# A channel-attention kernel whose two small warm-up tiles move from the front of the on-chip memory to its end

## The chip, the core and the metric

The kernel runs on one core of a Trainium2 chip. The core has a matrix engine (PE, with its weight loads listed apart as PEld), a vector engine (DVE), a scalar engine (ACT), a general engine (POOL) and a sync engine (SP) that here only issues transfers. All of them work on SBUF, an on-chip memory of 128 partitions; every buffer has one byte address that holds in all partitions. Sixteen DMA engines move data between HBM and SBUF. The metric is the device time of one execution in microseconds (us).

## The reference

Q, K and V have 8 batches, 12 heads, 512 rows and 64 columns in float32. For each of the 96 heads, Q and K are normalised along the rows, a 64 x 64 matrix of their products goes through a softmax, and V is multiplied by it:

```python
Q_norm = Q / (np.linalg.norm(Q, axis=-2, keepdims=True) + 1e-10)
K_norm = K / (np.linalg.norm(K, axis=-2, keepdims=True) + 1e-10)
attn = np.einsum('bhnd,bhne->bhde', Q_norm, K_norm)
attn = np.exp(attn - np.max(attn, axis=-1, keepdims=True))
attn = attn / (np.sum(attn, axis=-1, keepdims=True) + 1e-10)
return np.einsum('bhnd,bhde->bhne', V, attn).astype(np.float32)
```

Q, K and V are 12.6 MB each, and so is the result; all of it crosses the DMA engines once.

## The kernel before

**Work and staging.** Four heads make a unit (24 units), two units a step `s` (12 steps), and two steps a group `w` (6 groups). Q and K of a step land side by side in a float32 tile `qk32` (three buffers of 16 KB in each partition); V lands in `v32` (three of 8 KB). DVE casts Q and K to bfloat16 (`cast_qk`, L204); PE makes the products of a unit (`grams`, L224); DVE, ACT and POOL take the norms out of them, scale, and form the softmax (`squares` to `normalise`, L231 to L282); PE transposes V (`vtrans`, L293) and multiplies it by the weights (`outs`, L310); and ACT or DVE copies the result into a float32 tile `so` (`ocopy`, thirteen buffers of 4 KB), from which it is stored.

**Transfers.** All large transfers are issued by SP: `load_qk` (L180, L182, L184), `load_v` (L191, L193) and `store` (L198). A DMA packet carries one run of bytes that is contiguous in a partition and in HBM. From the shapes in those lines:

- Loads of V carry 8 KB in a packet, the last two 4 KB.
- Loads of Q and K carry 4 KB in a packet, those of the last unit 2 KB.
- Stores carry 2 KB in a packet (eight rows of 64 floats), the last two 1 KB.

**Order.** A small planner (`Order.run`) runs while the program is built. It holds a cost for each piece of work and writes out one order for each engine's queue. SP's queue is in order too; at most eight transfers are under way at a time, and the ninth waits for the first.

**The small reads.** Before everything else, ACT issues two transfers of 128 pieces of 64 bytes, one from Q and one from K, into two tiles `first0` and `first1`. No later instruction reads them.

**Addresses.** Buffers are given addresses in the order in which pools are opened and tiles are made in them. The first pool is `const`, and the tiles made first in it are `first0` and `first1`: they stand at bytes 16512 and 16576 and together take 128 bytes. Behind them come `ident`, `identb`, `eye2`, the four `ab` tiles, and then the other pools in the order of `NB`. A list of some of them:

| buffer | bytes in a partition | address before | remainder by 256 |
|---|---|---|---|
| first0, first1 | 64 each | 16512, 16576 | 128, 192 |
| ident | 512 | 16640 | 0 |
| ab (four) | 1024 each | 17664 and on | 0 |
| qk32 (three) | 16384 each | 21760, 38144, 54528 | 0 |
| v32 (three) | 8192 each | 70912, 79104, 87296 | 0 |
| vb, qkb, vt | 8192, 4096, 8192 | 95488, 111872, 120064 and on | 0 |
| so (thirteen) | 4096 each | 136448 and on | 0 |
| scr, kq (two each) | 2048 each | 189696 and on | 0 |
| kqs (two) | 2048 each | 198080, 200128 | 192 |
| ex (two) | 1024 each | 202240, 203264 | 0 |

Within a `qk32`, `v32` or `so` buffer the runs of all packets begin at multiples of 1 KB, so the address of the buffer sets where each packet begins within a block of 256 bytes.

Of the kernel before, what the change touches and what calls it, by code (L numbers as in the profile page):

```python
# [8 lines left out]
F32 = mybir.dt.float32  # L9
# [4 lines left out]
D = 64  # L14
# [88 lines left out]
def kernel(  # L103
# [36 lines left out]
    const = ctx.enter_context(tc.tile_pool(name="const", bufs=1))  # L140
# [4 lines left out]
    vtp = ctx.enter_context(tc.tile_pool(name="vtp", bufs=NB["vt"]))  # L145
    sop = ctx.enter_context(tc.tile_pool(name="sop", bufs=NB["so"]))
    small = ctx.enter_context(tc.tile_pool(name="small", bufs=NB["sm"]))
    ps_v = ctx.enter_context(tc.tile_pool(name="ps_v", bufs=1, space=bass.MemoryType.PSUM))
    ps_l = ctx.enter_context(tc.tile_pool(name="ps_l", bufs=1, space=bass.MemoryType.PSUM))
    ps_o = ctx.enter_context(tc.tile_pool(name="ps_o", bufs=2, space=bass.MemoryType.PSUM))  # L150
# [167 lines left out]


    for i in range(2):  # L320
        first = const.tile([128, D // 4], F32, name=f"first{i}")
        nc.scalar.dma_start(out=first, in_=(Q, K)[i][0, 0, :128, :D // 4])

    nc.scalar.add_instruction(mybir.InstLoadActFuncSet(
        name=nc.get_next_instruction_name(), engine=mybir.EngineType.Activation, ins=[], outs=[], act_func_set_id=LN_EXP))
# [102 lines left out]
    for s in range(S):  # L428
        for x in range(4):
            i, k = divmod(x, 2)  # L430
# [57 lines left out]
```

## Time and profile before

| what | value |
|---|---|
| median of 13 runs | 128.86 us (128.64 to 129.61) |
| the profiled execution's own time | 128.74 us |
| its span, first to last instruction | 127.0 us |
| DVE busy | 94.2 us (74% of the span) |
| PE busy, ACT busy, POOL busy | 72.9, 72.5, 38.6 us |
| DMA packets, bytes | 15893, 50.66 MB |
| mean DMA rate | 399 GB/s |
| share of 16 DMA engines' span taken by the large transfers' packets | 98.6% |

The span leaves out 1.74 us of the execution (128.74 less 127.0), which lies before its first and after its last instruction. In the slices of the page each digit stands for a fortieth of the span, 3.2 us; the rows named DMA and GB/s tell how busy the DMA engines were in it and how much they moved. In the list of DMA queues, q1 is SP's queue with the large transfers, q10 is ACT's with the two small reads, and q8 and q14 are fetches of the program itself.

### The profile page before, as it was taken

How to read it: one execution, taken by the hardware profiler on the slowest of the kernel's cores; microseconds unless marked ns; L12 is line 12 of the kernel's file. 1: busy time of each engine (PE TensorE's matmuls, PEld its weight loads, DVE VectorE, ACT ScalarE, POOL GpSimd, SP SyncE). 2: the span in 40 equal slices, each digit the busy share in tenths (PEclk: the TensorE clock that was granted, in tenths of full speed). 3: DMA queues.
4: the chain of work that ended last, by engine and by line, in shares of the span. 5: the costliest groups of instructions: out<-in, count | busy, mean ns of one | idle time of the engine just before them, and what ended most of it. 6: DMA issues, size and time to landing. Idle time of an engine off the chain costs nothing.

```text
span 127.0 us, 4885 instructions
## 1 busy us (share of the span) xinstructions
PE 72.9 (57%) x2128; PEld 59.1 (47%) x2128; DVE 94.2 (74%) x141; ACT 72.5 (57%) x220; POOL 38.6 (30%) x39
## 2 busy tenths in 40 slices
PE   0074087396583386855972689582977786853000
PEld 0063075285462275744852468371856574742000
DVE  3445756939999989997899999998999887960000
ACT  4000303557969209967386589877668997896000
POOL 4006307040833830432074301413473370300000
PEclk9999999999999558997799999999589997698555
DMA  4999999999999999999999999999999999999993
GB/s 136 378 431 418 421 416 418 416 428 413 422 427 413 413 414 426 403 421 421 428 412 416 410 425 418 416 431 414 408 407 417 397 407 399 404 403 407 407 373 127
DMA packets 15893, 50.66 MB, mean 399 GB/s; under 512 B 1408, under 2 KB 1920, under 8 KB 14464
## 3 DMA queue, kind: packets, MB, share of 16 engines
q1 hardware_dynamic: 15584, 50.34, 98.6%
q8 instruction: 16, 0.26, 0.7%
q10 hardware_dynamic: 288, 0.02, 0.2%
q14 instruction: 5, 0.04, 0.1%
HBM read 37.77 MB, written 12.58 MB: 397 GB/s over the span
## 4 chain that ended last, share of the span: by engine, by line
DVE 34%; PE 24%; issue 12%; DMA 11%; ACT 9%; POOL 1%; DVEq 0%; ACTq 0%; POOLq 0%
DVE qkb L204 16%; PE gram L224 12%; DMA qk<-in_K_dram 8%; DVE scr L231 6%; PE vps L293 5%; PE po L310 5%; DVE ab L282 5%; DVE vt L167 3%; DMA first<-in_Q_dram 3%; ACT so L165 3%; ACT vt L165 2%; PE lg L267 2%; ACT ex L273 2%; DVE n L243 2%; ACT kq L165 1%
## 5 line engine op out<-in xcount | busy, mean ns | idle before, releaser
L224 PE MATMUL gram<-qkb 32*128 32x128 bf16 (+1 forms) x1504 | 32.6, 242 | 28.1 <-DVE qkb L204 16.1
L204 DVE CAST qkb<-qk 128x1024 bf16<-128x1024 f32 x48 | 41.8, 897 | 5.6 <-DMA qk<-in_Q_dram 3.1
L224 PEld LDWEIGHTS <-qkb 32*128 32x128 bf16 (+1 forms) x1504 | 27.3, 107 | 32.3 <-DVE qkb L204 17.3
L169 POOL TENSOR_SCALAR vb<-v 128x1024 bf16<-128x1024 f32 x19 | 23.4, 1248 | 30.3 <-DMA v<-in_V_dram 29.4
L165 ACT COPY so<-po 128x512 f32<-128x512 f32 x45 | 24.9, 593 | 7.3 <-PE po L310 6.8
L254 POOL TENSOR_TENSOR kqs<-kq,r 64x512 f32<-64x512 f32 x12 | 13.9, 1158 | 40.4 <-issue 19.3
L165 ACT COPY vt<-vps 128x1024 bf16<-128x1024 bf16 (+1 forms) x18 | 17.8, 987 | 13.0 <-PE vps L293 12.8
L310 PE MATMUL po<-ab,vt 128*64 128x128 bf16 x384 | 19.4, 237 | 5.7 <-issue 1.8
L293 PE MATMUL vps<-identb,vb 128*128 128x128 bf16 x192 | 18.2, 248 | 7.1 <-DVE vt L167 2.5
L231 DVE SCALAR_TENSOR_TENSOR scr<-gram,eye 64x512 f32<-64x512 f32 x24 | 16.5, 688 | 5.8 <-PE gram L224 5.5
L293 PEld LDWEIGHTS <-vb 128*128 128x128 bf16 x192 | 13.9, 111 | 10.3 <-issue 6.2
L310 PEld LDWEIGHTS <-vt 128*64 128x64 bf16 x384 | 13.5, 118 | 10.2 <-issue 5.1
L273 ACT ACTIVATE ex<-lg,rq 128x64 f32<-128x64 f32 x48 | 14.5, 323 | 4.0 <-PE lg L267 4.0
L165 ACT COPY kq<-gram 64x512 f32<-64x512 f32 x12 | 7.0, 581 | 14.0 <-DVE scr L231 13.8
L282 DVE TENSOR_TENSOR ab<-ex,rinv 64x256 bf16<-64x256 f32 x24 | 12.3, 512 | 0.6
L273 ACT ACTIVATION_READ_ACCUMULATOR ex<-lg,rq 128x1 f32 x48 | 10.3, 214 | 0.0
L167 DVE COPY vt<-vps 128x1024 bf16<-128x1024 bf16 (+1 forms) x8 | 8.0, 1023 | 2.0 <-PE vps L293 1.9
L243 DVE TENSOR_REDUCE n<-scr 128x8 f32<-128x512 f32 x12 | 8.2, 680 | 0.1
L267 PE MATMUL lg<-eye,kqs 64*128 64x64 f32 x48 | 6.4, 258 | 1.9 <-POOL kqs L254 1.0
L267 PEld LDWEIGHTS lg<-eye,kqs 64*128 64x128 f32 x48 | 4.5, 156 | 3.6 <-issue 1.4
L167 DVE CAST vb<-v 128x1024 bf16<-128x1024 f32 x5 | 5.0, 1002 | 0.1
L279 DVE RECIPROCAL rinv<-esum 128x4 f32<-128x4 f32 x12 | 2.0, 170 | 3.9 <-ACT ex L273 3.9
(16 smaller groups left out, 15.8 us busy)
## 6 DMA issues: line engine op xcount, KB each, us to landing
out_dram<-so SPq DMA_DIRECT2D x23, 512.0 KB, 10.2
v<-in_V_dram SPq DMA_DIRECT2D x11, 1024.0 KB, 17.3
qk<-in_Q_dram SPq DMA_DIRECT2D x8, 1024.0 KB, 15.1
qk<-in_K_dram SPq DMA_DIRECT2D x8, 1024.0 KB, 16.9
qk<-in_Q_dram SPq DMA_DIRECT2D x8, 512.0 KB, 11.6
qk<-in_K_dram SPq DMA_DIRECT2D x8, 512.0 KB, 11.5
v<-in_V_dram SPq DMA_DIRECT2D x2, 512.0 KB, 10.7
out_dram<-so SPq DMA_DIRECT2D x2, 256.0 KB, 9.3
```

Of the source, the lines that this page charges most:

```text
L165: nc.scalar.copy(o, i)
L167: nc.vector.tensor_copy(o, i)
L169: nc.gpsimd.tensor_scalar(out=o, in0=i, scalar1=1.0, scalar2=0.0, op0=ALU.mult, op1=ALU.add)
L204: nc.vector.tensor_copy(qkb[u][:, :, x * D:(x + 1) * D], qk32[s][:, x, r])
L224: nc.tensor.matmul(gram[s][:, h, r, 0], x, x, start=(t == 0), stop=(t == (T if u < WIDE else J) - 1))
L231: nc.vector.scalar_tensor_tensor(out=scr[s][half], in0=gram[s][half, :, :, 0, half].rearrange("p h r d -> p (h r) d"), scalar=1e-20, in1=e ...
L254: (nc.vector if eng == "DVE" else nc.gpsimd).tensor_tensor(out=kqs[s][HI], in0=kq[s][HI], in1=r8[s][HI, :, None].to_broadcast([D, 2 * HU, ...
L267: nc.tensor.transpose(l[:, h, :], kqs[s][HI, 2 * h:2 * h + 2].rearrange("p r d -> p (r d)"), eye2[HI])
L273: nc.scalar.activation(e[:, h, :], lg[s][:, h, :], AF.Exp, scale=rq[s][:, h:h + 1], accum_out=z[:, h:h + 1])
L282: nc.vector.tensor_tensor(out=a[half, :, half], in0=e[half], in1=ri[half, :, None].to_broadcast([D, HU, D]), op=ALU.mult,)
L293: nc.tensor.transpose(ps[:, c, n, :], vb[w][:, J * c + j].rearrange("p r d -> p (r d)"), identb)
L310: nc.tensor.matmul(po[s, x][e * D:(e + 1) * D, j].rearrange("p r d -> p (r d)"), v, ab[s][:, h, :])
```

## The change

A new pool `endp` is opened behind `small`, the last pool of SBUF, and `first0` and `first1` are made in it and no longer in `const`:

```diff
     sop = ctx.enter_context(tc.tile_pool(name="sop", bufs=NB["so"]))
     small = ctx.enter_context(tc.tile_pool(name="small", bufs=NB["sm"]))
+    endp = ctx.enter_context(tc.tile_pool(name="endp", bufs=1))
     ps_v = ctx.enter_context(tc.tile_pool(name="ps_v", bufs=1, space=bass.MemoryType.PSUM))
...
     for i in range(2):
-        first = const.tile([128, D // 4], F32, name=f"first{i}")
+        first = endp.tile([128, D // 4], F32, name=f"first{i}")
         nc.scalar.dma_start(out=first, in_=(Q, K)[i][0, 0, :128, :D // 4])
```

All other buffers move down by 128 bytes: `ident` now stands at 16512, `qk32` at 21632, `v32` at 70784, `so` at 136320 and on. The remainders by 256 that were 0 are now 128; that of `kqs` goes from 192 to 64. The two small tiles stand at 204288 and 204352, with remainders 0 and 64. No engine's list of instructions changes, neither the order nor a shape nor what any instruction waits for.

## The prediction

> **What bounds the kernel now.** I read the slices first, then the DMA queues, then the chain of waits, and last the stretch in which nothing but stores is left. The slices of the page:
>
> ```profile
> DVE  3445756939999989997899999998999887960000
> DMA  4999999999999999999999999999999999999993
> GB/s 136 378 431 418 421 416 418 416 428 413 422 427 413 413 414 426 403 421 421 428 412 416 410 425 418 416 431 414 408 407 417 397 407 399 404 403 407 407 373 127
> ```
>
> DVE is busiest of the computing engines, but it has gaps and it is done four slices before the end. The DMA engines are at 9 in every slice but the first and the last. The queues say the same in one number:
>
> ```profile
> DMA packets 15893, 50.66 MB, mean 399 GB/s; under 512 B 1408, under 2 KB 1920, under 8 KB 14464
> q1 hardware_dynamic: 15584, 50.34, 98.6%
> q8 instruction: 16, 0.26, 0.7%
> q10 hardware_dynamic: 288, 0.02, 0.2%
> ```
>
> The packets of SP's transfers took 98.6% of what sixteen engines have in the span. The counts "under" are cumulative. Minus the 1408 tiny ones (the small reads and the completion marks), 512 packets are of 1 KB; 14464 less 1920 are of 2 or 4 KB; the rest, but for 21 fetches of the program, are the 1408 of 8 KB. With the shapes of the lines that is 6400 of 2 KB (5888 in stores, 512 in the last loads), 6144 of 4 KB, 1408 of 8 KB: in all 14464 packets that carry data, 904 for each engine. 6400 of them (5888 and 512) leave an `so` buffer, 8064 enter `qk32` or `v32`.
>
> The chain of waits tells another story at first sight:
>
> ```profile
> DVE 34%; PE 24%; issue 12%; DMA 11%; ACT 9%; POOL 1%; DVEq 0%; ACTq 0%; POOLq 0%
> ```
>
> It follows engine instructions through their semaphores, and a store that sits in a full queue has no place in it. What is decisive is the end. The stretches of 12 us (columns: time, length, busy time of PE, PEld, DVE, ACT, POOL, clock, DMA share, GB/s), and then a shorter one in the drain:
>
> ```profile
> 16.00:28.00 12.00, 8.77 (x232) 7.28 (x236) 7.72 (x13) 4.02 (x15) 3.69 (x3) 1.00 1.03 421
> ...
> 100.00:112.00 12.00, 9.16 (x200) 7.41 (x194) 9.59 (x17) 10.64 (x40) 4.55 (x4) 0.86 1.05 403
> ```
>
> ```profile
> 118.00:122.00 4.00, 0.00 (x0) 0.00 (x0) 0.00 (x0) 0.00 (x0) 0.00 (x0) 0.50 1.05 406
> ```
>
> In the last stretch no engine computes and only 2 KB (and the last 1 KB) stores run: the transfers that were queued drain, at the DMA engines' own pace. The last store is issued at 117.1 us and lands 9 us later. So the end is set by the sum of packet times on the DMA engines, from some 3 us on to 126, with hardly a hole. A packet that takes 1 ns longer moves the end by 904 ns if all are hit; a computing engine that gets faster or slower by little moves nothing.
>
> **What a packet costs.** The trace's packet records have nearly one time for each size: 11 ns for 64 bytes, 46 for 1 KB, 84 for 2 KB, 159 for 4 KB, 309 for 8 KB (medians). (309 - 159) ns for 4096 bytes are 1.172 ns for 32 bytes; I call that a beat. 9 ns and a beat for every 32 bytes fits all five. Neighbouring packets overlap by a few ns, which is why the DMA share above is over 1: at 406 GB/s an engine passes 25.4 bytes in a ns, so a 2 KB packet holds it for 80.7 ns. The completion marks take 16 x 9 ns for 256 packets of a store, 0.6 each; that leaves 80.1, of which 64 beats are 75.0 and 5.1 are the packet's own.
>
> **The change part by part.**
>
> Order, waits, issues: nothing. SP issues the same 70 transfers, ACT the same two small reads, ahead of the table load at L324 as before; nothing is added or moved on any queue. The pool at the end adds no wait, since nothing reads its tiles.
>
> The small reads' new places (0 and 64 in a block of 256 bytes, before 128 and 192): 256 packets of 11 ns on 16 engines are 0.18 us in total, while the first large loads are only starting. Were each 4 beats shorter or longer, it would be 16 x 4.7 = 75 ns. I take 0.
>
> The computing engines: every operand's address falls by 128 bytes, and the distances between buffers stay. The trace has no pair of one operation at both remainders. I bound it by the busiest row, DVE's 48 casts of 897 ns in the mean, 41.8 us: 1% either way is 0.4 us, hidden behind a DMA queue that had no hole even in 64 to 76 us, where DVE is busy for 11.8 of 12 us. To lose that cover the casts would have to slow so much that a load is issued late by more than the queue holds (a load of Q and K takes 11 to 17 us from issue to landing). I take 0.
>
> The packets' SBUF ends: this is where the change acts. All 14464 packets now begin 128 bytes into a block of 256 in SBUF; their ends in HBM stay. [...] I weigh it for the two directions.
>
> - *Stores* read SBUF. [...] 400 x 4.7 = 1.88 us. The trace holds no store from such an address; from below the price is 0 (the beats are hidden in the packet's own 5.1 ns), and a gain is bounded in the rivals.
> - *Loads* write SBUF; what they read in HBM is aligned as before. The nearest row is that of the small reads, q10 above: they do write at 128 and 192 bytes into a block, and take 11 ns, where the line through the other sizes gives 9 + 2 x 1.172 = 11.3. Had a write to pay for the bytes ahead of it, it would be 4.7 to 7 ns more, 16 to 18. So I take 0 for 8064 packets, against 504 x 4.7 = 2.36 us if loads paid like stores. The row doesn't settle it wholly: a 64-byte packet crosses no block, and a 4 KB one now touches 17 in place of 16. A beat for each additional block would be 504 x 1.172 = 0.59 us.
>
> The sum against the profiled execution's 128.74 us (span 127.0 and 1.74 around it): +1.88, so 130.6. The median of the runs shown is 0.12 above that execution; so 130.7. A second number follows for the drain: 80.7 + 4.7 = 85.4 ns for a packet, so some 384 GB/s where 406 stood.
>
> **The rivals.**
>
> *Loads pay too.* [...] Against it: the 11 ns of the small reads. 14464 packets, 904 on an engine, x 4.7 = 4.24 us: 133.1.
>
> *Only the additional block costs*, a beat or so on every packet: 904 x 1.172 = 1.06 us, 129.9. [...] Against it: nothing in the trace shows a beat for a block.
>
> *Nothing is seen*: the beats hide, and the kernel is not slower. [...] A 2 KB packet holds the engine for 80.1 / 1.172 = 68.3 beats, of which 64 move data[...]. The 4 additional beats fit into exactly that; it decides as soon as the surplus is 4.3 beats or less. [...] It gives 128.9[...].
>
> *Faster.* The packets' own 5.1 ns could become less at the new addresses. If one beat of it went on all packets, -1.06 us: 127.8. For it: I know of no row that says the old remainder is the best. Against it: five sizes lie on one line, and the 64-byte packets at other remainders lie on it too, so an effect of the old remainder on the fixed part isn't visible.
>
> *Far slower*: if each half-filled block broke the stream on both ends, 10 beats or more a packet, 904 x 11.7 = 10.6 us and more, over 139. Only possible, no row points to it.
>
> **How the numbers follow.** Stores pay 4 beats: 0.36. Loads too: 0.17. A beat for a block: 0.10. Far slower: 0.04. Nothing seen: 0.21. Faster: 0.12. The runs before can tell about 0.3% (0.4 us) from no change. Slower by more is 0.36 + 0.17 + 0.10 + 0.04 = 0.67, within it 0.21, faster 0.12. The likeliest is 130.7; its own range is 130.0 to 131.2 (room for one to two of the beats, or half a beat for the loads' blocks). The range of 8 in 10 has to reach down to no change and up to the case where loads pay as well: 128.5 to 133.3, which leaves out faster and far slower, 0.16.
>
> **What would show it.** Right: packets of 2 KB in the drain at about 384 GB/s, while the stretch from 16 to 28 us keeps its 421; a 2 KB packet of a store takes some 88 to 89 ns, and 4 and 8 KB ones stay at 159 and 309; the mean durations of casts, copies and matmuls stay. Wrong: 421 falls to some 410 early on (loads pay); 406 stays (nothing seen); a DMA row with holes while an engine's means have moved (then it's the computing engines, which I priced at nothing).

## The result, and the profile after

The changed kernel takes 130.35 us in the median (11 runs, 129.96 to 131.19); the kernel before, now over 48 runs, 129.06 us (128.62 to 130.05). The ratio is 1.011, with a 95% interval of 1.0086 to 1.0135: slower by 1.3 us. The profiled execution has 130.15 us and a span of 128.4, where the one before had 128.74 and 127.0.

The number is close to the forecast of 130.7, but the profile says that it came from elsewhere. The same rows as before, of the changed kernel; first the slices and the queues:

```profile
DVE  3443849919999989999977779999999789850000
DMA  4999999999999999999999999999999999999993
GB/s 128 392 435 408 421 407 406 408 420 405 411 425 407 403 407 411 404 415 424 414 412 407 415 417 421 405 429 405 405 408 403 398 402 403 401 406 408 407 363 116
DMA packets 15893, 50.66 MB, mean 395 GB/s; under 512 B 1408, under 2 KB 1920, under 8 KB 14464
q1 hardware_dynamic: 15584, 50.34, 98.4%
q8 instruction: 16, 0.26, 0.8%
q10 hardware_dynamic: 288, 0.02, 0.2%
```

Bytes and packets are the same, the DMA row is as full, and the mean rate has gone from 399 to 395 GB/s. So the same packets took longer. Which ones, the stretches tell (columns as before; the last number is GB/s):

```profile
16.00:28.00 12.00, 8.39 (x248) 7.16 (x244) 7.75 (x12) 4.70 (x15) 4.07 (x4) 0.77 1.03 411
...
118.00:122.00 4.00, 0.00 (x0) 0.00 (x0) 0.00 (x0) 0.00 (x0) 0.00 (x0) 0.50 1.05 408
```

In the drain, where only stores run, 408 GB/s stand where 406 stood: nothing is slower. Early on, where only loads run, 421 fell to 411. The forecast had these two the other way round. A longer stretch, almost wholly of loads, serves as the yardstick from here on; the kernel before, then the changed one:

```profile
28.00:52.00 24.00, 14.73 (x492) 12.04 (x480) 22.24 (x31) 16.07 (x51) 8.79 (x7) 0.86 1.02 418
```

```profile
28.00:52.00 24.00, 16.61 (x454) 13.62 (x443) 22.55 (x32) 15.76 (x51) 9.12 (x8) 0.71 1.02 411
```

The packet records put it in figures. "Late" is the share of packets over the common 84, 159 or 309 ns; "sum" is what all packets of that size took, divided by 16 engines.

| packets on SP's queue | before: mean, late, sum | after: mean, late, sum |
|---|---|---|
| 2 KB (stores, last loads) | 84.4 ns, 2%, 33.78 us | 84.7 ns, 6%, 33.87 us |
| 4 KB (loads) | 161.4 ns, 2%, 61.97 us | 163.2 ns, 38%, 62.65 us |
| 8 KB (loads) | 310.2 ns, 1%, 27.29 us | 314.6 ns, 59%, 27.68 us |

The differences of the sums are 0.09, 0.68 and 0.39, together 1.16 us for an engine, of the 1.4 by which the span grew. The loads bear 1.07 of it, and not as one surcharge on each packet: 62% of the 4 KB packets still take exactly 159 ns, nearly all others 160 to 172.

One execution of each kernel would not settle this by itself, for executions of one kernel spread by as much (128.62 to 130.05 us for the kernel before). The change shows in the medians, and in a stretch towards the end of the drain; the kernel before, then the changed one:

```profile
122.00:124.00 2.00, 0.00 (x0) 0.00 (x0) 0.00 (x0) 0.00 (x0) 0.00 (x0) 0.50 0.90 340
```

```profile
122.00:124.00 2.00, 0.00 (x0) 0.00 (x0) 0.00 (x0) 0.00 (x0) 0.00 (x0) 0.50 1.06 402
```

In the kernel before, some of the DMA engines are already done there (DMA share 0.90, where the drain had 1.05); in the changed one all are still at work (1.06). Of the other full kernels, shown below, the four whose load buffers start at multiples of 256 move 314 to 340 GB/s in these two microseconds, the two whose load buffers do not 391 and 404.

The chain of waits names the transfers now, because it happens to follow the stores at the end:

```profile
DMA 27%; PE 25%; DVE 25%; issue 8%; ACT 5%; SPq 1%; ACTq 0%; DVEq 0%
```

The row of the casts guards against a wrong reading of the computing engines; the kernel before, then the changed one:

```profile
L204 DVE CAST qkb<-qk 128x1024 bf16<-128x1024 f32 x48 | 41.8, 897 | 5.6 <-DMA qk<-in_Q_dram 3.1
```

```profile
L205 DVE CAST qkb<-qk 128x1024 bf16<-128x1024 f32 x48 | 37.9, 813 | 7.0 <-DMA qk<-in_Q_dram 4.7
```

The mean of the casts is 813 ns where it was 897; it is no mark of the addresses, since it goes from 759 to 905 ns in the kernels below, and 905 belongs to a kernel in which the casts' results have the changed remainder and their inputs the old one. PE's busy time rose from 72.9 to 78.8 us at a lower mean clock (0.800 for 0.892). Neither casts nor PE set the end: the DMA engines were full in both executions (98.6 and 98.4% of their time in the span went to packets of SP's queue).

### The profile page after: what moved, and what is told of

Read it like the earlier page. It is cut to its first block, busy times and chain, and to the rows that moved or that the text cites. A ratio compares the mean times of both kernels' runs of the same rounds, so it can differ in the third digit from the quotient of the medians.

```text
span 128.4 us, 4885 instructions
## 1 busy us (share of the span) xinstructions
PE 78.8 (61%) x2128; PEld 64.3 (50%) x2128; DVE 93.6 (73%) x141; ACT 72.5 (56%) x220; POOL 36.6 (29%) x39
## 3 DMA queue, kind: packets, MB, share of 16 engines
q1 hardware_dynamic: 15584, 50.34, 98.4%
## 4 chain that ended last, share of the span: by engine, by line
DMA 27%; PE 25%; DVE 25%; issue 8%; ACT 5%; SPq 1%; ACTq 0%; DVEq 0%
DMA out_dram<-so 21%; PE gram L225 14%; DVE qkb L205 10%; DVE scr L232 5%; DMA qk<-in_K_dram 5%; PE vps L294 5%; PE po L311 5%; DVE ab L283 4%; ACT so L166 3%; DVE n L244 2%; DVE vt L168 2%; PE lg L268 1%; ACT ex L274 1%; DVE so L168 1%; SPq L185 1%
## 5 line engine op out<-in xcount | busy, mean ns | idle before, releaser
L225 PE MATMUL gram<-qkb 32*128 32x128 bf16 (+1 forms) x1504 | 37.4, 264 | 24.5 <-DVE qkb L205 10.4
L225 PEld LDWEIGHTS <-qkb 32*128 32x128 bf16 (+1 forms) x1504 | 31.8, 119 | 29.0 <-DVE qkb L205 12.8
L205 DVE CAST qkb<-qk 128x1024 bf16<-128x1024 f32 x48 | 37.9, 813 | 7.0 <-DMA qk<-in_Q_dram 4.7
L170 POOL TENSOR_SCALAR vb<-v 128x1024 bf16<-128x1024 f32 x19 | 21.7, 1153 | 39.5 <-DMA v<-in_V_dram 35.3
L166 ACT COPY vt<-vps 128x1024 bf16<-128x1024 bf16 (+1 forms) x18 | 17.7, 986 | 16.9 <-PE vps L294 16.7
L311 PE MATMUL po<-ab,vt 128*64 128x128 bf16 x384 | 20.6, 248 | 5.3 <-issue 2.9
L311 PEld LDWEIGHTS <-vt 128*64 128x64 bf16 x384 | 14.5, 124 | 10.0 <-issue 6.3
L283 DVE TENSOR_TENSOR ab<-ex,rinv 64x256 bf16<-64x256 f32 x24 | 15.1, 631 | 0.6
L168 DVE CAST vb<-v 128x1024 bf16<-128x1024 f32 x5 | 5.5, 1096 | 0.1
```

The costliest lines, as they stand in the source:

```text
L166: nc.scalar.copy(o, i)
L168: nc.vector.tensor_copy(o, i)
L170: nc.gpsimd.tensor_scalar(out=o, in0=i, scalar1=1.0, scalar2=0.0, op0=ALU.mult, op1=ALU.add)
L205: nc.vector.tensor_copy(qkb[u][:, :, x * D:(x + 1) * D], qk32[s][:, x, r])
L225: nc.tensor.matmul(gram[s][:, h, r, 0], x, x, start=(t == 0), stop=(t == (T if u < WIDE else J) - 1))
L283: nc.vector.tensor_tensor(out=a[half, :, half], in0=e[half], in1=ri[half, :, None].to_broadcast([D, HU, D]), op=ALU.mult,)
```

## The experiments

All addresses below were moved by empty tiles placed ahead of a pool (and a second one behind it, to bring what follows back to its old remainder). "Off the block" means that a buffer starts some bytes behind a multiple of 256. Ratios are to the kernel before, run on the same chip in the same session (129.09, 129.57 and 129.28 us in the three sessions). The kernels without computing are compared with one another by their times. The last four of them ran in a later session and on another chip than the first two; the very last, whose packets were all on time, gives a base there (127.01 us beside 127.05).

**Which buffers? Four kernels.** The small reads alone behind everything, with a gap of 128 bytes in their old place:

```diff
     const = ctx.enter_context(tc.tile_pool(name="const", bufs=1))
+    const.tile([128, 32], F32, name="gap")
...
-        first = const.tile([128, D // 4], F32, name=f"first{i}")
+        first = endp.tile([128, D // 4], F32, name=f"first{i}")
```

> The small reads stand behind all other buffers, and a gap of 128 bytes takes their old place, so that every other buffer keeps its old address. Theory that a packet which loads into SBUF from 128 bytes into a block is at times delayed: ratio 1.000 (within 0.002), 8 KB packets at a mean of 310 ns as before. Rival that the place of the small reads matters: 1.010.

Measured: 129.1 us against 129.09, ratio 0.9999 (0.9979 to 1.002); 8 KB packets at a mean of 310.5 ns. Its profiled execution is one of the longer ones (130.03 us), and yet its loads run as before:

```profile
28.00:52.00 24.00, 18.39 (x488) 15.55 (x490) 18.02 (x30) 16.22 (x50) 8.89 (x8) 0.71 1.02 418
```

Where the small reads stand is of no account; the move matters through the addresses of the others alone. It also shows the cure: the order of the buffers costs nothing here once a gap restores the remainder.

Only the load buffers off the block:

```diff
+    gap0 = ctx.enter_context(tc.tile_pool(name="gap0", bufs=1))
+    gap0.tile([128, 32], F32, name="gap0_t")
     qp = ctx.enter_context(tc.tile_pool(name="qp", bufs=NB["qk"]))
     vp = ctx.enter_context(tc.tile_pool(name="vp", bufs=NB["v"]))
+    gap1 = ctx.enter_context(tc.tile_pool(name="gap1", bufs=1))
+    gap1.tile([128, 32], F32, name="gap1_t")
     vbp = ctx.enter_context(tc.tile_pool(name="vbp", bufs=NB["vb"]))
```

> Only qk32 and v32, which the loads fill, start 128 bytes into a block of 256; all else stays at remainder 0. Loads theory: the whole effect, ratio 1.009 to 1.012, 4 KB packets at a mean of 163 ns and 8 KB ones at 314 to 315, stretch 16 to 28 us near 411 GB/s. Stores theory (the one of the prediction): 1.000. Rival that the computing engines' other operands count: 1.000.

Measured: 130.57 us, ratio 1.0105 (1.0063 to 1.0148): the whole effect. 4 KB packets had a mean of 162.8 ns (38% late), 8 KB ones 314.5 (58% late). Its stretches:

```profile
28.00:52.00 24.00, 17.78 (x489) 14.68 (x478) 20.47 (x32) 16.41 (x52) 9.02 (x8) 0.71 1.02 411
118.00:122.00 4.00, 0.00 (x0) 0.00 (x0) 0.00 (x0) 0.00 (x0) 0.00 (x0) 0.50 1.05 408
```

Only the store buffers off the block (the same two gaps, ahead of `sop` and of `small`):

> Only the so buffers, which the stores read, start 128 bytes into a block. Stores theory of the prediction: ratio 1.010 to 1.015, the drain at 384 GB/s in place of 406. Loads theory: 1.000 (within 0.002), 2 KB packets at 84 ns, the drain at 406.

Measured: 129.21 us, ratio 1.0005 (0.9979 to 1.003); 2 KB packets 84 ns in the median and 84.7 in the mean. The drain and the loads are both as before:

```profile
28.00:52.00 24.00, 16.32 (x464) 13.48 (x467) 19.82 (x31) 16.71 (x53) 10.23 (x8) 0.75 1.02 418
118.00:122.00 4.00, 0.00 (x0) 0.00 (x0) 0.00 (x0) 0.00 (x0) 0.00 (x0) 0.53 1.05 407
```

All but the transferred buffers off the block (the changed kernel, with gaps ahead of `qp`, `vbp`, `sop` and `small`):

> qk32, v32 and so keep remainder 0; every other buffer (the casts' and transposes' results, the constants, the small tiles of the softmax) has its remainder moved by 128 as in the change. Loads theory and stores theory: ratio 1.000 (within 0.002). Rival that operands of the computing engines count, through traffic that disturbs the DMA's writes: 1.005 to 1.010.

Measured: 128.99 us, ratio 0.9994 (0.9969 to 1.0019). The computing engines' operands don't count.

```profile
28.00:52.00 24.00, 14.74 (x497) 12.06 (x495) 21.85 (x30) 16.10 (x50) 9.55 (x7) 0.86 1.02 418
```

The yardstick stands at 411 where the loads' buffers are off the block and at 418 where they aren't.

**Does the delay need the computing engines? Two kernels** in which SP issues all transfers in the planner's order and nothing is computed:

```diff
     for (emit, eng), (_, _, key, _) in zip(plan.run(), plan.order):
-        if eng == "DMA" and not passed and (held or key == HELD):
-            held.append(emit)
-            continue
-        emit(eng)
-        ...
+        if eng == "DMA":
+            emit(eng)
```

> All loads and stores in SP's order at their old addresses, with the computing left out: the stores send zeroed buffers, and no engine works but the zeroing at the start. Base for the next run. All theories: 2 KB, 4 KB and 8 KB packets at 84, 159 and 309 ns, time 125 to 128 us, the limit that the DMA engines set.

Measured: 127.05 us (127.0 to 127.1, 4 runs).

> As the run before it, computing left out, but qk32 and v32 start 128 bytes into a block. Theory A, the delay arises among the DMA engines' own writes: 4 KB packets again at a mean of 163 ns and 1.1 to 1.3 us more than with the old addresses. Theory B, it needs engines that read and write SBUF beside the writes (a collision in the memory): no packet delayed, time equal to the run before within 0.2 us.

Measured: 128.36 us (127.73 to 128.6, 10 runs), 1.31 more. 49% of the 4 KB packets were late (mean 163.4 ns), 71% of the 8 KB ones (314.3). Theory B fell. The first, then the second kernel (columns here: time, length, DVE, ACT, POOL, clock, DMA share, GB/s):

```profile
28.00:52.00 24.00, 0.00 (x0) 0.00 (x0) 0.00 (x0) 1.00 1.02 422
```

```profile
28.00:52.00 24.00, 0.00 (x0) 0.00 (x0) 0.00 (x0) 1.00 1.03 415
```

With every other engine idle and the clock at 1.00 throughout, the gap between the two is 7 GB/s, as in the full kernels. So the delay arises in the transfers themselves.

**Which starts pay? Three kernels.** Load buffers 64 bytes into a block (gaps of 16 and 48 floats in place of 32 and 32):

> qk32 and v32 start 64 bytes into a block, all else at remainder 0. If any start off a block of 256 costs, by one more block in each packet: ratio 1.009 to 1.012 as with 128. If the price goes with the bytes ahead of the start (2 beats in place of 4): about 1.005. If only half blocks cost: 1.000.

Measured: 130.67 us, ratio 1.0093 (1.0057 to 1.013), 53% and 88% late. As dear as 128 (410 GB/s in the yardstick).

Load buffers at multiples of 512 (gaps of 64 and 64 floats):

> qk32 and v32 start at multiples of 512, where before they start at odd multiples of 256. If blocks of 256 count: ratio 1.000 (within 0.002), packets at 159 and 309. If blocks of 512 count and the old addresses pay already: faster, 0.990 to 0.997.

Measured: 129.23 us, ratio 0.9986 (0.9958 to 1.0013), 2% and 2% late. The yardstick is at 418. A step of 256 bytes cost nothing, so blocks of 512 don't count here. No trace holds an absolute address; what these runs test are steps away from the old place, of which 64 and 128 bytes cost time (1.0093 and 1.0105), as 32 do in the next run (128.6 us beside 127.05), and 256 does not.

Transfers alone, 32 bytes into a block (gaps of 8 and 56 floats):

> Transfers alone, load buffers 32 bytes into a block. If any start off a block costs alike: 128.3 us as with 128 (127.05 with the old addresses). If the price went with the bytes ahead of the start: 127.4.

Measured: 128.6 us (127.91 to 128.86, 16 runs), beside 128.36 with 128 bytes. The price does not go with the bytes ahead of the start.

**Does each packet pay for itself? Three kernels** without computing. The changed loads all in one row to a partition (`ONE = S` for `ONE = 3`):

> Transfers alone, computing left out, load buffers 128 bytes into a block; all loads of Q and K but the last unit's now carry one row of 4 KB in a partition (512 KB), as only those of the first steps did, in which few packets were delayed; the planner also puts nearly all loads ahead of the stores. If the delay needs the two-row transfers: packets at 159 and 309 nearly everywhere, 127.0 to 127.4 us. If it comes up whenever loads have run alone for some 15 us: 4 KB packets at a mean of 163 or more, 128.3 us or more.

Measured: 128.32 us (127.93 to 128.89, 12 runs), 56% and 80% late. The shape of the loads isn't what spared the early ones.

Only `qk32` off the block (gaps ahead of `qp` and of `vp`):

> Transfers alone, only qk32 at 128 bytes into a block (two thirds of the load bytes), v32 at 0. If each packet from such a start pays for itself: 4 KB packets delayed, 8 KB packets at 309, 127.05 plus some 0.9, 127.9 to 128.0. If a shared path is at its limit and all writers wait: 8 KB packets delayed too.

Measured: 127.87 us (127.75 to 128.03, 4 runs), 0.82 over the aligned transfers (0.86 over the next kernel, run beside it). 37% of the 4 KB packets were late; the 8 KB ones, on the block, hardly (9%, mean 309.6).

Only `v32` off the block (gaps ahead of `vp` and of `vbp`):

> Transfers alone, only v32 at 128 bytes into a block, qk32 at its old address. If each packet pays for itself: 8 KB packets at a mean of 316, 4 KB ones at 159, 127.05 plus 0.4. If a shared path is at its limit: 4 KB packets delayed too.

Measured: 127.01 us (126.87 to 127.16, 4 runs), nothing over the aligned transfers; 1% of the 8 KB packets late, mean 309.2. A miss: 0.4 us had been expected. Its yardstick is that of aligned loads:

```profile
28.00:52.00 24.00, 0.00 (x0) 0.00 (x0) 0.00 (x0) 1.00 1.02 422
```

So the prices don't add up. Off-block loads of V cost nothing among on-block ones of Q and K (127.01), yet when all loads are off the block 71% of the same 8 KB packets are late. The records point the same way. In the run with only `qk32` off the block, from 17 us of the span on, 61% of the 4 KB packets were late where no other size ran within 1 us of them, 36% where 8 KB packets ran beside them, 13% among 2 KB ones; with both off the block those were 64%, 66% and 27%. In the first 15 us of the span only 8 to 13% of the 4 KB packets were late in the runs with all load buffers at 64 or 128 bytes, beside 7% in the kernel before; with 32 bytes and with `ONE = S` it was 32% and 29%, still less than half of what followed. Packets that enter none of these buffers lose time too: the sixteen fetches of the program (q8) took 16.7 or 16.8 us together in the three full kernels with off-block loads, 14.9 in the five others. Why the share of late packets goes with what runs beside them and before them, and why a late load loses mostly between 1 and 13 ns (97% of the late 4 KB packets of the changed kernel, 96% of its late 8 KB ones), no run shows.

## Why the prediction was right, and where not

- *The bound* held: the DMA engines' packet times set the end (98.4% of the span on SP's queue). 1.16 us more for each engine became 1.4 us of span. Of the remaining 0.2, the program's fetches give 0.12 (16.8 us in all for 14.9, on sixteen engines). That single profiles agree so well is partly chance, given the spread of the runs.
- *Orders, waits, the small reads' place and computing engines at nothing*: right. A kernel with the small reads' move alone and one with all other operands off the block both came out at 1.000 within 0.003.
- *Stores, +1.88 us*: wrong, this is the step that failed. 4 beats (4.7 ns) for each of 400 packets on an engine were the whole of the forecast. That a store pays them was the author's assumption, which no row of the trace had shown, and no run showed it: the drain went from 406 to 408 GB/s where 384 were forecast, a 2 KB packet took 84.7 ns in the mean where 88 to 89 were, and stores alone gave 1.0005 (0.9979 to 1.003). The rival "nothing is seen" had the stores right; whether for its reason, that the beats hide in the packet, can't be told from the runs.
- *Loads, 0, with 2.36 us as the upper end*: wrong as well; they cost about 1.07 us. The argument rested on the 64-byte packets that took 11 ns at 128 and 192 bytes into a block. That row was true and could not tell. The prediction saw one possible reason itself: a 64-byte packet there crosses no block, and a beat for each additional block (0.59 us) was then left out of the sum. Another is the time, though no run parts the two: these packets run between 2.3 and 5.2 us of the span, and in the changed kernel too 90% of the 4 KB loads of the first 15 us were on time. A row of short, early packets was taken for a rule on long runs.
- *The two errors partly cancelled*: 1.88 too much for the stores, 1.07 too little for the loads. The forecast was a rise of 1.84 us (128.86 to 130.7), the measured one is 1.29; the totals lie closer, 0.35 apart, because the median of the kernel before came out 0.20 higher over 48 runs than over the 13 that the prediction had. That the total came close is luck. The likeliest case, at 0.36, was not what happened. The rivals "loads pay too" and "a beat for a block" (1.06 us on all packets) come near in size or place, but in neither do the stores go free.
- *What would show it* did its work: "421 falls to some 410 early on (loads pay)" is what the stretch from 16 to 28 us shows, and "406 stays (nothing seen)" what the drain shows.

## What to carry to other kernels

Where the DMA queue is full from end to end, look at the addresses of the buffers that loads fill: here starts 64 and 128 bytes off a multiple of 256 cost 0.9 and 1.05%, and a small tile more or less ahead of them can bring it about; a gap that restores the remainder took it back (ratio 0.9999). Read a stretch in which only one kind of transfer runs, since a total that comes out as forecast does not show that its terms did. And a price taken from a few short packets should be tried on a long run before it is used for one.

## What the runs showed of the hardware that was not expected

- Loads into SBUF from 32, 64 or 128 bytes into a block of 256 were all slowed alike (4 KB packets from a mean of 160 to 162 ns to one of 163 or 164). Stores from 128 bytes into a block were not slowed by more than the runs can tell, 0.3% (2 KB packets 84.7 ns in the mean, 84.4 before). Multiples of 512 gained nothing over odd multiples of 256 (0.9986, 0.9958 to 1.0013).
- The slowing isn't additive: with transfers alone it costs 0.82 us for Q and K off the block, 0 for V, 1.31 for both.
- Packets that enter none of the moved buffers were slower in the full kernels with off-block loads: the program's fetches took 16.7 or 16.8 us in all for 14.9.
- The computing of the whole kernel added only some 2.5 us to its transfers: they took 127.05 us by themselves, the whole kernel 129.57 in the same session.
